# Six of nine input projections by one level of Strassen's product, with weight sums formed in DRAM

## Chip, core and metric

The kernel runs on one core of one Trainium2 chip. TensorE (PE in the profile) multiplies, VectorE (DVE), ScalarE (ACT) and GpSimd (POOL) do the elementwise work, SyncE (SP) and POOL issue most of the DMAs, and all DMAs share the core's 16 DMA engines. The metric is device time of one launch in microseconds (us), the median of three runs.

## What is computed

The reference is one layer of a hybrid decoder on 1024 tokens of width 1024, with 16 learned meta tokens put in front. Cut to what matters here:

```
h = rmsnorm(concat(meta, x))                       # 1040 x 1024
glu_a, glu_b, z, q, f, i, g_rec, m_conv, m_rec = split(h @ W_in)    # nine projections, 1024 x 1024 each
y_conv = (silu(layernorm(dwconv31(glu_a * sigmoid(glu_b)))) * silu(z)) @ W_conv_out
y_rec  = (group_rmsnorm(hgrn2(q, f, i)) * gnorm_g * silu(g_rec)) @ W_rec_out
x = x + (sigmoid(m_conv) * y_conv + sigmoid(m_rec) * y_rec) @ W_out
out = rmsnorm(x) * final_g
```

All of it is float32. hgrn2 is a gated linear recurrence over 8 heads.

## The kernel before, in words

Activations lie transposed: features on the 128 partitions, tokens along the row, eight k-tiles `hh[k]` of 1040 columns. A float32 product is made of three matmuls on rounded parts: every operand x is split into `hi` (x rounded to the type float32r) and `lo` = x - hi, and a product is hi·hi + hi·lo + lo·hi. `project` (L292 on) computes one 128-wide output tile over all tokens: for each column block it runs 8 k-tiles times these three matmuls (L300, L303, L304) into one PSUM bank. Tiles that also need the meta tokens (f, glu_a, glu_b) use the blocks `FB` of 348, 346 and 346 columns, the others `RB`, two blocks of 512.

The program is a list of jobs, one per output tile, and each job is a generator. In order of the program: v quarter 0 and 1 (from x itself, before the norm is known), then for head j = 0..7 the tiles f_j and q_j, with v quarter 2 after head 1 and v quarter 3 after head 3; then glu_b and glu_a of tile 0, and then, mixed by a counter, the eight g_rec tiles (`g_job`), the m_rec tiles with the W_rec_out tiles (`mr_job`, `ro_job`) and the other seven glu pairs; then z with the layer norm's statistics, m_conv (`mc_job`), W_conv_out (`co_job`), and last the product with W_out, whose lines are L907 to L909.

Each weight tile is loaded by SP in one DMA of 512 KB (`load_w`, L136), rounded by ACT (L126), negated by ACT (L127), and `lo` is completed by a DMA of POOL that adds the raw weights onto it in place (`split_dma`, L128, "wlo<-wraw"). Two raw buffers and three split buffers make a lookahead of one job.

Two background queues are advanced while matmuls are issued. `tick` takes a step of `hgrn` (the recurrence of one head: matmuls of tile "hg", DVE products) every `HG_GAP` us of matmul work, and `CONV_RATE` steps of `conv_taps` per us, each a DVE operation of 1024 columns (L612); `hgrn` ends with the normalised output `o_n` (L508), and `g_job` transposes it (L643). All the gates (m_rec, z, m_conv) stay in SBUF slots until they are used. The order of each engine's instructions is fixed when the program is built; an engine works through its own in that order and waits where an operand is not there.

Of the kernel before, what the change touches and what calls it, by code (L numbers as in the profile page):

```python
# [33 lines left out]
LN_AT = 3  # L34


@with_exitstack
def hybrid_kernel(ctx: ExitStack, tc: tile.TileContext, xT, xtok, wv, wp, wro, wco, wout, prm, fg, msk, out):
# [5 lines left out]
    qx = ctx.enter_context(tc.tile_pool(name="qx", bufs=2))  # L44
    wpool = ctx.enter_context(tc.tile_pool(name="wpool", bufs=3))
# [105 lines left out]
    def load_x(k):  # L151
# [6 lines left out]
        cuts = (0, NM + 2 * P, L) if k == 0 else (0, L)  # L158
# [22 lines left out]
    def v_mm(ps, k, c, ws, hi, lo, pair, first, last, shared):  # L181
# [6 lines left out]
        if c < NC:  # L188
            p0 = NM + c * P
# [31 lines left out]
    for c in range(NC):  # L221
        pe.matmul(pb[:, c:c + 1], lhsT=s2[:, NM + c * P:NM + (c + 1) * P], rhs=inv[:, 0:1], start=True, stop=True)
# [66 lines left out]
    for b, ps in enumerate(bcast_tok(diag_tok(rtok[:, 0:8]))):  # L289
        act.copy(out=rbc[:, NM + b * 512:NM + (b + 1) * 512], in_=ps)  # L290

    def project(w, xh, xl, blocks):  # L292

        whi, wlo = w
        res = []
        for o, n in blocks:
            ps = mm_bank()
            for k in range(KT):
                ks = slice(k * P, (k + 1) * P)
                mm = pe.matmul(ps[:, 0:n], lhsT=whi[:, ks], rhs=xh[k][:, o:o + n], start=(k == 0), stop=False)  # L300
                if not res and k == 0:
                    marks.append(mm)
                pe.matmul(ps[:, 0:n], lhsT=whi[:, ks], rhs=xl[k][:, o:o + n], start=False, stop=False)  # L303
                pe.matmul(ps[:, 0:n], lhsT=wlo[:, ks], rhs=xh[k][:, o:o + n], start=False, stop=(k == KT - 1))  # L304
                unit[0] = 3 * n / 2400.0
                if k < KT - 1:
                    yield None
            res.append(ps)
            yield o, n, ps

    on = [None] * NC
# [36 lines left out]
    def hgrn(j, Fg, K, QD):  # L348
# [21 lines left out]
        PA = slot("PA")  # L370
# [12 lines left out]
        QY = qx.tile([P, 7, 256], F32, name="QY", tag="qx")  # L383
        QY4 = QY.rearrange("p s (b u) -> p s b u", u=8)
# [102 lines left out]
        o_n = slot(f"o{j}", T)  # L487
        on[j] = o_n
# [22 lines left out]
        done.add(j)  # L511


    hh, hl, hpair = [], [], []
    jobs = []

    def normalise():
        hs = []
        for k in range(KT + 1):
            if k < KT:  # L520
# [3 lines left out]
                hs.append(h)  # L524
                hh.append(slot(f"hh{k}", dt=F32R))
# [7 lines left out]
    done = set()  # L533

    def f_job(j):
        def run(w):
            Fg = slot("F")
            K = slot("K")
# [14 lines left out]
    def q_job(j):  # L553
        def run(w):
            QD = qx.tile([P, 3, 512], F32, name="QD", tag="qx")
            for blk in project(w, hh, hl, RB):
# [4 lines left out]
                h0 = (o - NM) // 2  # L561
# [17 lines left out]

    def gb_job(j):  # L580
        def run(w):
            sg = slot("gsig")
# [9 lines left out]
    def ga_job(j):  # L592
        def run(w):
            a = glu.pop(j)
            for blk in project(w, hh, hl, FB):
                yield
                if blk is None:
# [3 lines left out]
            cj = slot(f"c{j}", T)  # L601
            conv[j] = cj
            dve.tensor_scalar(out=cj, in0=a[:, NM:L], scalar1=cw[:, j, TAPS - 1:TAPS], scalar2=conv_b[:, j:j + 1],
                              op0=ALU.mult, op1=ALU.add)
            cbg.append(conv_taps(j, a, cj))
# [18 lines left out]

    def c_reload():
# [5 lines left out]
    rh, rl = [], []  # L631

    def g_job(j):
        def run(w):
            while j not in done:
                step(bg)
            rec = slot("rec", T)
            po = []
            for b in range(2):
                ps = hg_bank()  # L640
                for c in range(4):
                    s = (4 * b + c) * P
                    pe.transpose(ps[:, c * P:(c + 1) * P], on[j][:, s:s + P], ident)  # L643
                po.append(ps)
            i = -1
            for blk in project(w, hh, hl, RB):
                yield
                if blk is None:
                    continue
                o, n, ps = blk  # L650
                i += 1
                sg = rec[:, i * 512:(i + 1) * 512]
                act.activation(out=sg, in_=ps, func=AF.Silu)
                dve.scalar_tensor_tensor(out=rec[:, i * 512:(i + 1) * 512], in0=po[i], scalar=gnorm[:, j:j + 1],
                                         in1=sg, op0=ALU.mult, op1=ALU.mult)
            hi = slot(f"rh{j}", T, F32R)
            lo = slot(f"rl{j}", T, F32R)
            split(rec, hi, lo)
            rh.append(hi)
            rl.append(lo)  # L660
        return run

    gate = {}
    grec_d = dram.tile([KT, P, T], F32, name="grec_d")
    c_d = dram.tile([KT, P, T], F32, name="c_d")
    gmc = {}

    def mr_job(j):
        def run(w):
            sm = slot("smr", T)  # L670
            for blk in project(w, hh, hl, RB):
                yield
                if blk is None:
                    continue
                o, n, ps = blk
# [197 lines left out]
    for _ in nrm:  # L873
        pass
# [158 lines left out]
```

## Time and profile before

| | us |
|---|---|
| median of 3 runs | 1233.21 (1232.68 to 1233.66) |
| the profiled execution | 1233.92 |
| its span, first to last instruction | 1231.9 |
| PE busy in it | 1203.6 |
| DVE busy | 753.3 |
| ACT busy | 420.6 |
| POOL busy | 140.7 |

The profile is of one execution. Busy time of an engine is the time in which it has an instruction running; matmuls overlap, so a matmul's own duration is longer than its pitch, the distance from one start to the next. "DMA share" is the mean busy share of the 16 DMA engines in a stretch.

### The profile page before, as it was taken

How to read it: one execution, taken by the hardware profiler on the slowest of the kernel's cores; microseconds unless marked ns; L12 is line 12 of the kernel's file. 1: busy time of each engine (PE TensorE's matmuls, PEld its weight loads, DVE VectorE, ACT ScalarE, POOL GpSimd, SP SyncE). 2: the span in 40 equal slices, each digit the busy share in tenths (PEclk: the TensorE clock that was granted, in tenths of full speed). 3: DMA queues.
4: the chain of work that ended last, by engine and by line, in shares of the span. 5: the costliest groups of instructions: out<-in, count | busy, mean ns of one | idle time of the engine just before them, and what ended most of it. 6: DMA issues, size and time to landing. Idle time of an engine off the chain costs nothing.

```text
span 1231.9 us, 19297 instructions
## 1 busy us (share of the span) xinstructions
PE 1203.6 (98%) x8136; PEld 1048.3 (85%) x8136; DVE 753.3 (61%) x1232; ACT 420.6 (34%) x722; POOL 140.7 (11%) x187
## 2 busy tenths in 40 slices
PE   8999999999999999999999999999999999999997
PEld 7988898997888889898989898888878788888886
DVE  7555736736766894778695969587651601435444
ACT  7553233343334333233222222221352824332211
POOL 5330010010001001010011101101100000110000
PEclk9999999999999999999999999999999999999999
DMA  5242142132222233343544444444634244654421
GB/s 217 84 115 58 36 103 69 36 85 69 55 69 70 54 83 94 97 103 86 138 107 115 120 120 103 133 107 127 183 87 100 65 106 103 162 130 161 147 86 52
DMA packets 35383, 124.22 MB, mean 101 GB/s; under 512 B 3936, under 2 KB 4320, under 8 KB 35296
## 3 DMA queue, kind: packets, MB, share of 16 engines
q0 software_dynamic: 17440, 63.51, 23.5%
q1 hardware_dynamic: 17712, 59.32, 14.0%
q8 instruction: 64, 1.05, 0.3%
q14 instruction: 23, 0.19, 0.1%
q10 hardware_dynamic: 144, 0.16, 0.0%
HBM read 67.40 MB, written 11.53 MB: 64 GB/s over the span
## 4 chain that ended last, share of the span: by engine, by line
PE 89%; DVE 8%; ACT 1%; issue 1%; DMA 0%; SPq 0%; DVEq 0%; ACTq 0%
PE mm L300 23%; PE mm L303 23%; PE mm L304 23%; PE mm L191 2%; PE mm L193 2%; PE mm L192 2%; PE mm L908 1%; PE mm L907 1%; PE mm L909 1%; PE hg L907 1%; PE hg L908 1%; PE hg L909 1%; PE hg L480 1%; PE hg L497 1%; PE hg L496 1%; DVE QX L367 1%
## 5 line engine op out<-in xcount | busy, mean ns | idle before, releaser
L300 PE MATMUL mm<-hh,whi 128*128 128x512 f32 (+2 forms) x1216 | 443.0, 365 | 0.0
L303 PE MATMUL mm<-hl,whi 128*128 128x512 f32 (+2 forms) x1216 | 439.5, 361 | 0.0
L304 PE MATMUL mm<-hh,wlo 128*128 128x512 f32 (+2 forms) x1216 | 438.1, 360 | 0.0
L612 DVE SCALAR_TENSOR_TENSOR c<-gsig,pt,c 128x1024 f32<-128x1024 f32 (+7 forms) x240 | 307.2, 1280 | 6.8
L300 PEld LDWEIGHTS mm<-hh,whi 128*128 128x128 f32 x1216 | 229.5, 189 | 29.4 <-ACT whi L126 0.5
L304 PEld LDWEIGHTS mm<-hh,wlo 128*128 128x128 f32 x1216 | 229.3, 189 | 28.0
L303 PEld LDWEIGHTS mm<-hl,whi 128*128 128x128 f32 x1216 | 229.4, 189 | 27.7 <-issue 0.5
L126 ACT CAST whi<-wraw 128x1024 fp32r<-128x1024 f32 x84 | 88.1, 1049 | 362.3 <-PE mm L303 349.1
L128 POOL DMA_DIRECT2D wlo<-wraw x84 | 73.1, 870 | 740.2 <-ACT wlo L127 651.1
L127 ACT ACTIVATE wlo<-whi 128x1024 fp32r<-128x1024 f32 x84 | 88.6, 1055 | 0.9
L600 DVE TENSOR_TENSOR gsig<-gsig,mm 128x346 f32<-128x346 f32 (+1 forms) x24 | 12.4, 516 | 84.8 <-PE mm L304 84.8
L565 DVE TENSOR_TENSOR QD<-mm,QD 128x512 f32<-128x512 f32 x16 | 18.0, 1123 | 59.4 <-ACT QD L564 59.4
L123 DVE TENSOR_TENSOR cl<-sz,ch 128x1024 fp32r<-128x1024 f32 x8 | 9.4, 1221 | 67.3 <-ACT ch L122 67.3
L304 PE MATMUL mm<-rh,wlo 128*128 128x512 f32 x128 | 50.5, 394 | 0.0
L300 PE MATMUL mm<-rh,whi 128*128 128x512 f32 x128 | 50.4, 394 | 0.0
L303 PE MATMUL mm<-rl,whi 128*128 128x512 f32 x128 | 50.4, 394 | 0.0
L303 PE MATMUL mm<-cl,whi 128*128 128x512 f32 x128 | 50.3, 394 | 0.0
L304 PE MATMUL mm<-ch,wlo 128*128 128x512 f32 x128 | 50.1, 393 | 0.0
L300 PE MATMUL mm<-ch,whi 128*128 128x512 f32 x128 | 50.0, 393 | 0.0
L191 PE MATMUL mm<-whi,xhi 128*128 128x256 f32 x112 | 33.0, 302 | 5.5 <-ACT xhi L162 5.5
L191 PE MATMUL mm<-whi,hh 128*128 128x256 f32 x128 | 37.5, 293 | 0.0
L192 PE MATMUL mm<-wlo,hh 128*128 128x256 f32 x128 | 36.0, 281 | 0.0
(261 smaller groups left out, 1701.0 us busy)
## 6 DMA issues: line engine op xcount, KB each, us to landing
wlo<-wraw POOLq DMA_DIRECT2D x84, 512.0 KB, 4.6
wraw<-in_wp_dram SPq DMA_DIRECT2D x64, 512.0 KB, 3.3
wraw<-in_wro_dram SPq DMA_DIRECT2D x8, 512.0 KB, 3.4
grec_d<-smr POOLq DMA_DIRECT2D x8, 512.0 KB, 3.0
wraw<-in_wco_dram SPq DMA_DIRECT2D x8, 512.0 KB, 3.3
gr<-grec_d POOLq DMA_DIRECT2D x8, 512.0 KB, 6.3
wraw<-in_wout_dram SPq DMA_DIRECT2D x8, 512.0 KB, 3.7
xt<-in_xtok_dram POOLq DMA_DIRECT2D x8, 512.0 KB, 5.8
```

What stands on the lines that cost most here:

```text
L126: act.copy(out=hi, in_=src)
L127: act.activation(out=lo, in_=hi.bitcast(F32), func=AF.Copy, scale=-1.0)
L128: nc.gpsimd.dma_start(out=lo, in_=src, accum_op=ALU.add)
L191: pe.matmul(ps, lhsT=a, rhs=whi, start=first, stop=False, **kw)
L192: pe.matmul(ps, lhsT=a, rhs=wlo, start=False, stop=False, **kw)
L193: mm = pe.matmul(ps, lhsT=b, rhs=whi, start=False, stop=last, **kw)
L300: mm = pe.matmul(ps[:, 0:n], lhsT=whi[:, ks], rhs=xh[k][:, o:o + n], start=(k == 0), stop=False)
L303: pe.matmul(ps[:, 0:n], lhsT=whi[:, ks], rhs=xl[k][:, o:o + n], start=False, stop=False)
L304: pe.matmul(ps[:, 0:n], lhsT=wlo[:, ks], rhs=xh[k][:, o:o + n], start=False, stop=(k == KT - 1))
L612: dve.scalar_tensor_tensor(out=dst, in0=a[:, p0 - d:L - d], scalar=cw[:, j, TAPS - 1 - d:TAPS - d], in1=dst, op0=ALU.mult, op1=ALU.add)
L907: pe.matmul(ps, lhsT=a, rhs=whi, start=(k == 0), stop=False)
L908: pe.matmul(ps, lhsT=a, rhs=wlo, start=False, stop=False)
```

## The change

The two projections that the same hidden tokens feed are taken in pairs: glu_b with glu_a, g_rec with m_rec, z with m_conv. For a pair and a tile j, the weights form a 2 x 2 block matrix (projection by upper and lower half of the 1024 features), the activations another (feature half by token half). One level of Strassen's product in Winograd's form gives the four blocks from 7 block products where the plain way takes 8. `strassen` runs the seven, each of 4 k-tiles times the three matmuls, and combines them with TT (elementwise operations of DVE) on PSUM and on work tiles; `put` is handed the four results and turns them into gates.

Weight sums: each pair needs four sums of weight blocks, 128 x 512 each (256 KB). `weight_sums` forms them in DRAM: for each batch of two or three tiles four copies DRAM to DRAM on SP's queue (L714), and four DMAs on POOL's queue that add onto them (L716), in three dependent stages. 23 pairs (glu 1 to 7, rec 0 to 7, z 0 to 7) make 11 batches, 44 copies and 44 additions.

Activation sums: `normalise` also writes h to DRAM (L552); at the beginning of the Strassen part `h_sums` loads it again, forms four combinations per k on DVE (L796 to L799) and splits them with ACT and POOL's adding DMA.

Gates and outputs: rec (the normalised recurrence output times silu(g_rec)), sigmoid(m_rec), silu(z), sigmoid(m_conv) go to DRAM and come back when used; the transposes of o_n moved from `g_job` into the end of `hgrn` (L535), whose result goes to DRAM too. The token axis has 16 columns twice (1056 columns, two halves of 528), so f and glu 0 now use four blocks of 264, 264, 256 and 256 columns. The order of parts is now: f, q, v and glu 0, all recurrence steps and weight sums drained, then 23 Strassen units, then W_rec_out, layer norm, W_conv_out and the last product.

```diff
-FB = ((0, 348), (348, 346), (694, 346))
-RB = ((16, 512), (528, 512))
-SLOTS = 37
+FB = ((0, 264, 0), (264, 264, 264), (LH + NM, 256, LH), (LH + NM + 256, 256, LH + 256))
+RB = ((NM, 512, 0), (LH + NM, 512, 512))
+SLOTS = 35
-HG_GAP = 2.1
-CONV_RATE = 0.7
-GLU_OVER = 22
+HG_GAP = 1.85
+CONV_RATE = 0.57
+SUM_GAP = 3.6
+GLU_OVER = 15
...
+        count[2] += unit[0]
+        if count[2] >= SUM_GAP:
+            count[2] = 0.0
+            step(sbg)
...
+            s = [sums[kind][i, j0:j1].rearrange("j p n -> p j n") for i in range(4)]
+            a = {(r, h): blk(kind, r, h, j0, j1) for r in range(2) for h in range(2)}
+            batches.append((
+                ((s[0], a[1, 0]), (s[2], a[1, 0]), (s[1], a[0, 0]), (s[3], a[0, 1])),
+                ((s[0], a[1, 1]), (s[2], a[0, 0])),
+                ((s[1], s[0]),),
+                ((s[3], s[1]),)))
+        for t in range(len(batches) + 3):
+            for st in range(4):
+                if 0 <= t - st < len(batches):
+                    for dst, src in batches[t - st][st]:
+                        if st == 0:
+                            nc.sync.dma_start(out=dst, in_=src)
+                        else:
+                            nc.gpsimd.dma_start(out=dst, in_=src, accum_op=ALU.add)
+                        yield
...
+    drain(bg)
+    drain(sbg)
+    first.close()
...
+    def h_sums():
+        for k in range(4):
+            ha, hb = slot("ha"), slot("hb")
+            nc.sync.dma_start(out=ha, in_=h_d[k])
+            nc.sync.dma_start(out=hb, in_=h_d[k + 4])
...
+            TT(out=t56[:, 0], in0=b11, in1=b12, op=ALU.subtract)
+            TT(out=t56[:, 1], in0=t56[:, 0], in1=b22, op=ALU.add)
+            TT(out=t74[:, 0], in0=b22, in1=b12, op=ALU.subtract)
+            TT(out=t74[:, 1], in0=t56[:, 1], in1=b21, op=ALU.subtract)
+            for i, src in ((6, t56[:, 1]), (5, t56[:, 0]), (4, t74[:, 1])):
+                t = slot(f"t{i}_{k}", dt=F32R).rearrange("p (a n) -> p a n", a=2)
+                split_dma(src, t[:, 0], t[:, 1])
+                tt[i].append(t)
+            split_dma(t74[:, 0], hh[k][:, LH:LX], hl[k][:, LH:LX])
...
+        def product(i, ps, mov, start=True):
+            whi, wlo = take(m0 + i)
+            for c, (o, n) in enumerate(cols):
+                for k in range(4):
+                    a, b = whi[:, k * P:(k + 1) * P], wlo[:, k * P:(k + 1) * P]
+                    xh, xl = (m[:, o:o + n] for m in mov(k))
+                    mm = pe.matmul(ps[c], lhsT=a, rhs=xh, start=start and k == 0, stop=False, skip_group_check=True)
...
+                    pe.matmul(ps[c], lhsT=a, rhs=xl, start=False, stop=False, skip_group_check=True)
+                    pe.matmul(ps[c], lhsT=b, rhs=xh, start=False, stop=k == 3, skip_group_check=True)
...
+        yield from product(0, X, b11)
...
+        yield from product(1, W, tcomb(6))
...
+        yield from product(2, X, b21, False)
...
+        yield from product(3, Y, t7)
...
+        yield from product(4, Z, tcomb(5))
...
+        yield from product(5, Y, tcomb(4), False)
...
+        yield from product(6, Z, b22, False)
```

How the engines' orders move, at the places that matter. First the beginning of SP's queue, where x and the first weights are loaded ("x" is the input, "wraw" raw weights). Before:

```order
L136 DMA wraw<-in_wv_dram 128x768
L160 DMA x_122<-in_xT_dram 128x1040
L160 DMA x_131<-in_xT_dram 128x1040
L136 DMA wraw<-in_wv_dram 128x1024
L160 DMA x_146<-in_xT_dram 128x1040
L160 DMA x_155<-in_xT_dram 128x1040
```

And with the change:

```order
L147 DMA wraw<-in_wv_dram 128x768
L714 DMA sum_rec<-in_wp_dram 128x2x512 x2
L171 DMA x_122<-in_xT_dram 128x1056
L714 DMA sum_rec<-in_wp_dram 128x2x512 x2
L171 DMA x_131<-in_xT_dram 128x1056
L147 DMA wraw<-in_wv_dram 128x1024
L714 DMA sum_glu<-in_wp_dram 128x2x512
L171 DMA x_146<-in_xT_dram 128x1056
L714 DMA sum_glu<-in_wp_dram 128x2x512 x2
```

The copies of the weight sums stand between the loads of x, and all 44 of them stand ahead of the load of q_2's weights. Second, POOL's queue from the splits of q_1 to those of f_2 ("wlo<-wraw" is the adding DMA that completes a weight's low part). Before:

```order
L128 DMA wlo<-wraw 128x1024 x2
L459 COPY km<-K 128x32
L355 MEMSET attnd 128x256
L128 DMA wlo<-wraw 128x1024 x2
L353 MEMSET attn 128x1024
```

With the change, where the first split shown is that of the second half of v quarter 2 and the last that of f_2:

```order
L716 DMA sum_z<-in_wp_dram 128x2x512 x2
L716 DMA sum_z<-sum_z 128x2x512
L716 DMA sum_rec<-sum_rec 128x2x512
L477 COPY km<-K 128x32
L716 DMA sum_z<-in_wp_dram 128x2x512 x2
L372 MEMSET attnd 128x256
L716 DMA sum_z<-sum_z 128x2x512 x2
L139 DMA wlo<-wraw 128x1024
L716 DMA sum_z<-in_wp_dram 128x2x512 x2
L716 DMA sum_z<-sum_z 128x2x512 x5
L370 MEMSET attn 128x1024
L139 DMA wlo<-wraw 128x1024
```

All 44 additions now stand ahead of the split of f_2's weights, 18 of them ahead of that of f_0. Third, DVE behind the last block of glu 0 ("c_5339" is the convolution of tile 0, "on" the normalised output of head 7, "ha" and "hb" the reloaded h), with the change:

```order
L112 TENSOR_TENSOR rt_o<-rt_o,rh_o 128x8
L645 SCALAR_TENSOR_TENSOR c_5339<-glu,pt,c_5339 128x1024
L113 SCALAR_TENSOR_TENSOR ro<-rt_o,ry_o 128x8
L645 SCALAR_TENSOR_TENSOR c_5339<-glu,pt,c_5339 128x1024
L525 TENSOR_TENSOR on<-hg,ro 128x512 x2
L645 SCALAR_TENSOR_TENSOR c_5339<-glu,pt,c_5339 128x1024 x3
L645 SCALAR_TENSOR_TENSOR c_5339<-glu,pt,c_5339 128x1023
L796 TENSOR_TENSOR t_5434<-ha 128x528
L798 TENSOR_TENSOR t_5435<-hb,ha 128x528
L797 TENSOR_TENSOR t_5434<-t_5434,hb 128x528
L645 SCALAR_TENSOR_TENSOR c_5339<-glu,pt,c_5339 128x1022
L799 TENSOR_TENSOR t_5435<-t_5434,hb 128x528
```

Before, that work on DVE held nothing of PE: its order behind the last matmuls of head 7 ("S", "Q") was

```order
L496 MATMUL hg<-v_2503,attn 128x128
L300 MATMUL mm<-hh_681,whi 128x512
L497 MATMUL hg<-S,Q 128x128
L303 MATMUL mm<-hl_682,whi 128x512
L304 MATMUL mm<-hh_681,wlo 128x512
```

with the transposes of head 7's output some 600 matmuls later, inside its g_rec tile. With the change it is

```order
L514 MATMUL hg<-S,Q 128x128
L535 MATMUL hg<-ident,on 128x128 x8
L841 MATMUL hg<-hh_582,wh 128x512
L844 MATMUL hg<-hl_583,wh 128x512
L845 MATMUL hg<-hh_582,wl 128x512
```

The transposes of head 7's output, which waits for DVE, now stand ahead of the first Strassen matmul. From the start of that convolution (one L613) to the "on" rows DVE has 13 convolution steps (L645) and 12 small operations of eight columns, from there to the last of the 16 operations of `h_sums` another 17 convolution steps.

## Rows read from the trace of the kernel before

**Rows 1.** The page: busy time of the engines, and the chain's shares by engine.

```profile
PE 1203.6 (98%) x8136; PEld 1048.3 (85%) x8136; DVE 753.3 (61%) x1232; ACT 420.6 (34%) x722; POOL 140.7 (11%) x187
PE 89%; DVE 8%; ACT 1%; issue 1%; DMA 0%; SPq 0%; DVEq 0%; ACTq 0%
```

**Rows 2.** PE's timeline in three stretches, start and duration in us first.

```profile
979.67 0.39 PE L300 MATMUL mm<-hh,whi 128*128 128x512 f32 x1
...
983.85 0.40 PE L300 MATMUL mm<-hh,whi 128*128 128x512 f32 x1
...
70.13 0.32 PE L303 MATMUL mm<-hl,whi 128*128 128x346 f32 x1
...
73.93 0.32 PE L303 MATMUL mm<-hl,whi 128*128 128x346 f32 x1
...
54.55 0.28 PE L193 MATMUL mm<-whi,xlo 128*128 128x256 f32 x1
...
57.95 0.28 PE L192 MATMUL mm<-wlo,xhi 128*128 128x256 f32 x1
```

**Rows 3.** Windows: busy us by engine, granted clock, DMA share, GB/s.

```profile
core 0: us, PE busy (x) PEld busy (x) DVE busy (x) ACT busy (x) POOL busy (x), PEclk, DMA share, GB/s
0.00:62.00 62.00, 56.24 (x430) 53.92 (x431) 40.39 (x58) 39.40 (x68) 30.15 (x38) 1.00 0.43 149
0.00:160.00 160.00, 149.16 (x1463) 138.53 (x1464) 98.64 (x195) 77.77 (x155) 44.73 (x57) 1.00 0.34 98
```

**Rows 4.** Line L192 between 118 and 166 us: v quarter 2.

```profile
L192 PE MATMUL mm<-wlo,hh x64: 276/280/293, 121.3 to 156.3; 128*128 128x256 f32 x64
```

**Rows 5.** Windows around one adding DMA, one weight load, and the loads of x.

```profile
456.00:460.00 4.00, 4.00 (x19) 3.24 (x18) 4.00 (x5) 1.85 (x3) 0.00 (x0) 1.00 0.69 131
460.00:464.00 4.00, 4.00 (x19) 3.24 (x18) 3.93 (x5) 0.00 (x0) 0.00 (x0) 1.00 0.37 133
10.00:15.00 5.00, 5.00 (x30) 4.89 (x30) 4.07 (x4) 5.00 (x6) 2.88 (x4) 1.00 1.03 421
```

**Rows 6.** The page's DMA issues: KB each, us from issue to landing.

```profile
wlo<-wraw POOLq DMA_DIRECT2D x84, 512.0 KB, 4.6
```

**Rows 7.** DVE's timeline at 575 us, then groups: busy us, mean ns.

```profile
574.96 11.84 DVE L612 SCALAR_TENSOR_TENSOR c<-gsig,pt,c 128x1024 f32<-128x1024 f32 x9
L600 DVE TENSOR_TENSOR gsig<-gsig,mm 128x346 f32<-128x346 f32 x16 | 8.3, 516 | 49.0 <-PE mm L304 49.0
L603 DVE TENSOR_SCALAR c<-gsig,pt 128x1024 f32<-128x1024 f32 x8 | 6.5, 813 | 0.3
L101 DVE TENSOR_TENSOR rt_o<-rt_o,rh_o 128x8 f32<-128x8 f32 x24 | 4.0, 165 | 0.6
L508 DVE TENSOR_TENSOR o<-hg,ro 128x512 f32<-128x512 f32 x16 | 10.3, 685 | 0.4
L449 DVE TENSOR_TENSOR K<-K,PA 128x512 f32<-128x512 f32 x16 | 11.0, 690 | 10.3 <-PE hg L443 9.5 <-PE hg L435 0.8
L122 ACT CAST mh<-gr 128x512 fp32r<-128x512 f32 x16 | 9.8, 615 | 42.0 <-DVE gr L790 42.0
```

**Rows 8.** Window from head 6 to the last product.

```profile
300.00:1060.00 760.00, 755.67 (x4471) 652.30 (x4470) 498.20 (x632) 255.02 (x377) 71.23 (x93) 1.00 0.40 102
```

More of the change, by code (lines that the diff above doesn't have):

```diff
@@ L524, in normalise @@
                 hs.append(h)
+                nc.gpsimd.dma_start(out=h_d[k], in_=h)
                 hh.append(slot(f"hh{k}", dt=F32R))
@@ new lines, in add_pair, with add_plain, take_tile @@
+    def add_pair(kind, j, fn):
+        units.append((len(pieces), fn))
+        a = {(r, h): wp[SECT[kind][r], j][:, h * 512:(h + 1) * 512] for r in range(2) for h in range(2)}
+        s = [sums[kind][i, j] for i in range(4)]
+        pieces.extend([a[0, 0], s[1], a[0, 1], s[2], s[0], a[1, 1], s[3]])
+    def add_plain(srcs, fn):
+        units.append((len(pieces), fn))
+        for src in srcs:
+            pieces.extend([src[:, 0:512], src[:, 512:1024]])
+    def take_tile(m):
+        a, b = take(m), take(m + 1)
+        return (a[0], b[0]), (a[1], b[1])
@@ L625, in c_reload, with rec_reload @@
+    rh, rl = [], []
+    def rec_reload():
+        for k in range(KT):
+            r = slot(f"r{k}", T)
+            nc.sync.dma_start(out=r, in_=rec_d[k])
+            hi, lo = slot(f"rh{k}", T, F32R), slot(f"rl{k}", T, F32R)
+            split_dma(r, hi, lo)
+            rh.append(hi)
+            rl.append(lo)
     def c_reload():
@@ L629, in c_reload @@
             conv[j] = cj
[L631 to L660, printed above, removed]
-        return run
@@ L663, in hybrid_kernel @@
[L663 to L675, printed above, removed]
-                act.activation(out=sm[:, o - NM:o - NM + n], in_=ps, func=AF.Sigmoid)
-            gate[j] = sm
-        return run
@@ L870, in hybrid_kernel @@
-    for i, _ in enumerate(v1):
-        if i % 6 == 0:
-            next(nrm, None)
-    for _ in nrm:
-        pass
-    def execute(job):
-        fn, w = job
-        for _ in fn(w):
-            tick()
-    pending = None
-    for srcs, fn in jobs:
-        ws = [load_w(s) for s in srcs]
-        if pending is not None:
-            execute(pending)
-        pending = (fn, ws[0] if len(ws) == 1 else ws)
-    execute(pending)
+    order = []
+    nglu = 1
+    for i in range(16):
+        order.append(("rec", i) if i < 8 else ("z", i - 8))
+        if (i + 1) * 7 // GLU_OVER >= nglu and nglu < KT:
+            order.append(("glu", nglu))
+            nglu += 1
@@ new lines, in hybrid_kernel @@
+    for kind, j in order:
+        if kind == "glu":
+            add_pair(kind, j, glu_unit(j))
+        elif kind == "rec":
+            add_pair(kind, j, gate_unit(rec_d, gmr_d, j, True))
+        else:
+            add_pair(kind, j, gate_unit(sz_d, gmc_d, j, False))
+    add_plain([], simple(rec_reload))
+    add_plain([wro[0], wro[1]], ro_first(0))
+    add_plain([], simple(c_reload))
+    for j in range(2, KT):
+        if j == LN_AT:
+            add_plain([], simple(lambda: drain(cbg)))
+            add_plain([], simple(ln_stats))
+        if j == LN_AT + 3:
+            add_plain([], simple(ln_var))
+        if j == LN_AT + 4:
+            add_plain([], simple(ln_bcast))
+            add_plain([], simple(ln_apply))
+        add_plain([wro[j]], ro_unit(j))
@@ L890, in hybrid_kernel @@
+    for j in range(KT):
+        add_plain([wco[j]], co_unit(j))
+    h_sums()
+    for m0, fn in units:
+        for _ in fn(m0):
+            tick()
     fgt = slot("fgt", T)
```

456 lines of the change are left out of this document (305 added, 151 removed).

## Prediction

> **What bounds the kernel now.** I read the page first: PE is busy for 98% of the span, and 89% of the chain that ended last runs through it [rows 1]. The busy time alone would not prove a bound, because matmuls overlap, so the second view is PE's timeline, where the pitch shows [rows 2]. The 512-column matmuls start 18 pitches apart in 4.18 us, 0.2322 us each; 24 pitches of 346 columns take 3.80 us, 0.1583 each; 29 of 256 columns take 3.40 us, 0.1172 each. They follow each other without a hole, so a matmul that is left out gives its pitch back, as long as nothing else becomes late. The third view is the windows. From 300 to 1060 us PE is busy for 755.67 of 760 us, with DVE at 498 us and a DMA share of 0.40 [rows 8]; there PE is the bound and all else has room. The first 160 us are the part to study for this change: there the DMA share is 0.34 [rows 3], so of 160 us the 16 engines are idle for 106 and busy for 54. The reader should keep that 106.
>
> **The matmuls removed.** A rec or z pair takes 96 matmuls of 512 columns now and 84 then: 12 x 0.2322 = 2.79 us, times 16 pairs is 44.6 us. A glu pair takes 144 matmuls of 346 (22.80 us) and then 168 of 264. No row has 264 columns; between the rows of 256 and 346 the pitch is 0.1172 + 8 x 0.0411 / 90 = 0.121 us, so 20.31 us; 2.49 x 7 = 17.4 us. The ten f and glu 0 tiles go from 72 x 0.1583 = 11.40 us to 48 x 0.121 + 48 x 0.1172 = 11.43: +0.3 us in all. The transposes of the heads are moved, not added. **Sum on PE: -61.7 us**, all of it in stretches where PE is the bound.
>
> **The weight sums added.** 23 pairs x 4 sums x 256 KB are 24.1 MB copied DRAM to DRAM and 24.1 MB added onto DRAM, each as much as 46 DMAs of 512 KB. The price of such a DMA is not in the trace, because none goes from DRAM to DRAM. The nearest rows are windows with one DMA in them [rows 5]: an adding DMA of 512 KB from SBUF to SBUF holds all 16 engines for 0.69 x 4 = 2.76 us, a load of 512 KB for 0.37 x 4 = 1.48 us. At these prices: 46 x 1.48 + 46 x 2.76 = 195 us. The other end comes from the traffic: the most that the trace shows DRAM deliver is 421 GB/s, at a DMA share of 1.03 [rows 5]. A copy reads and writes a byte, an addition reads two and writes one, so 24.1 x 2 + 24.1 x 3 = 120.5 MB at 421 GB/s is 286 us. To either comes h written to DRAM, eight times 541 KB, 12 us.
>
> What that costs is decided by where it stands. In the new order all 44 additions stand on POOL's queue ahead of the split of f_2's weights, and 43 of the 44 copies ahead of their load on SP's, so PE cannot begin f_2 before nearly all of it is through. Now f_2 begins behind the last matmul of v quarter 2, at 157 us or a little later [rows 4]; I take 160. Up to there 106 us of DMA time are idle. If every idle moment is filled, the delay is 195 + 12 - 106 = 101 us by the low price and 286 + 12 - 106 = 192 us by the high one. No row decides between them: the low price leaves out that both ends are in DRAM, the high one that reads alone were measured. I take the middle, **+147 us**. A part shows early. 18 additions and 17 copies stand ahead of f_0, which needs 27 us of DMA time now (0.43 of 62, [rows 3]); with 18 x 2.76 + 17 x 1.48 = 75 us more and the first h it is ready at about 107 us at the low price, not 62. The copies also stand between the loads of x, in a stretch where the engines are full already [rows 5].
>
> The Trainium skill says more of a copy's price: the page "DMA: Bandwidth & Descriptors", section "Latency and other measured facts", has copies between HBM tensors at 207 to 214 GB/s in each direction. No run here shows that; my estimate from the page is 24.1 MB / 0.21 = 115 us for the copies where the load's row gives 68, and a delay of 148 us where the low end gives 101.
>
> **The start of the Strassen part.** Here the new order makes PE wait for DVE. Behind PE's last glu 0 matmul DVE has the evacuation (0.52), the start of the convolution (0.81), 13 convolution steps of 11.84 / 9 = 1.31 us, 12 small operations of 0.165 and the two "o" operations of 0.69 [rows 7]: 0.5 + 0.8 + 17.0 + 2.0 + 1.4 = 21.7 us. PE has about one us of work in that time, eight small matmuls, and then the transposes that need "on". Wait: 20 us. Before, the same DVE operations stood there and the transposes far later, so nothing waited. Then DVE has 17 more convolution steps (22.3 us) and the 16 sums of h_sums (16 x 0.69 = 11.0) before the last t is formed; two ACT operations of 0.62 [rows 7] and an adding DMA that lands in 4.6 us [rows 6] follow: 39 us. PE can do three products that need no sum and three quarters of four that do, 36 + 36 = 72 matmuls, 16.7 us. Wait: 22 us. **Together +43 us**, on the path by PE's order. Below, it could be 20, if the sums are formed earlier than I read; above, hardly more than 50.
>
> **The rest.** A rec pair then takes PE 84 x 0.2322 = 19.5 us. In that time DVE has some ten convolution steps (13.4) and seven operations of 0.69 (4.8), 18.2 us, and the DMA engines seven half-size pieces at (1.48 + 2.76) / 2, four stores of half size and one load, 14.8 + 3.0 + 1.5 = 19.3 us. What had room [rows 8] is now within 7% of PE in three places. Waits will appear; I book 10 us for the section and the reload of rec, with 0 and 46 (a tenth of the section's 458 us) as ends. In W_conv_out the normalised tiles come from DVE in about 2.4 us each, and two tiles' matmuls, mixed by k, use one in 2.8 us: nothing.
>
> **The sum** is made against the profiled execution, 1233.9 us (2 us beside its span; the median of the runs is 0.7 us less): 1233.9 - 61.7 + 147 + 43 + 10 = **1372 us**.
>
> **Rivals.**
> *The sums are hidden, and it is faster.* They are needed only by the first products, after all of f, q and v, and the engines are idle for two thirds of the first 160 us. Against it: f_2 stands behind them in POOL's queue, and the prices. The point from which it decides: copy and addition of 512 KB together below (106 - 12) / 46 = 2.04 us, where the rows give 4.24. Then 1233.9 - 61.7 + 43 + 10 = 1225 us. 9%.
> *The sums delay, but the start of the Strassen part does not wait*, because the long waits for weights let DVE and the loads run ahead. Against it: the convolution starts only behind PE's last glu matmul. 1372 - 43 = 1329 us. 8%.
> *The Strassen units are bound by DMA or DVE, not by PE.* For it: 19.3 and 18.2 us against 19.5, and the sums' pieces arrive as bursts of seven. Then another 45 us: 1417 us. 13%.
> *Fewer matmuls than seven for eight are saved*: excluded, since the new order holds 84 and 168 per unit.
>
> **How the numbers follow.** My forecast has 70%; its own range, by the two prices, is 1326 to 1417 us. The range that should hold the time 8 times in 10 reaches down past the second rival to cheap sums and a short start, and up past the third: 1255 to 1455 us. A measurement of this kernel tells about 0.2% from no change. Faster by more: the first rival's, nearly all of its 9%, 8%; within 0.2%: 1%; slower: 91%.
>
> **What would show it.** In the changed profile: a DMA share near 1 over the first 200 us and more; PE waiting for wlo's DMA at f_0 and above all at f_2, which begins past 250 us; nothing of the kind after it; then PE waiting for DVE's "on" and for t6, t5, t7 for some 40 us; pitches as before, 0.232 for 512 columns and about 0.121 for 264; and a rec unit in 19.5 to 21 us. The prediction is wrong if f_2 begins before 200 us (the sums are cheaper than both prices), if the PE's wait at the first transposes is under 10 us, or if units take over 22 us.

## The result, and the profile after

The changed kernel takes 1419.2 us (median of 4, 1416.5 to 1421.3), the kernel before 1232.95 in the same session: ratio 1.151 [1.149, 1.153]. It is slower, by 186 us; the prediction had 1372 (1255 to 1455). The profiled execution took 1416.5 us. First its page: PE's busy time, granted clock and DMA share in 40 slices of 35.4 us.

```profile
PE 1204.5 (85%) x8352; PEld 1030.4 (73%) x8352; DVE 835.0 (59%) x1422; ACT 624.4 (44%) x1130; POOL 317.6 (22%) x410
...
PEclk8677877999999999659999999999998799999999
DMA  9998999552042212999999999999999897656331
```

PE was busy for 1203.6 us before [rows 1] and for 1204.5 now, although some 60 us of matmuls are gone: a first hint that the remaining ones became slower. The clock row says where: in the first seven slices and at two later places. The windows show the stages (columns as in [rows 3]).

```profile
0.00:160.00 160.00, 84.31 (x538) 78.16 (x538) 53.82 (x76) 50.36 (x83) 50.96 (x80) 0.76 1.00 269
160.00:260.00 100.00, 71.61 (x815) 62.56 (x816) 42.83 (x114) 22.36 (x52) 27.75 (x28) 0.80 1.07 238
260.00:560.00 300.00, 283.46 (x3270) 257.44 (x3269) 171.04 (x464) 110.40 (x293) 26.10 (x41) 1.00 0.29 73
560.00:640.00 80.00, 38.82 (x106) 24.05 (x105) 52.63 (x65) 38.85 (x74) 27.98 (x33) 0.66 0.90 218
640.00:1074.00 434.00, 434.00 (x2427) 377.53 (x2426) 348.03 (x393) 295.89 (x468) 133.58 (x158) 1.00 0.97 236
1074.00:1140.00 66.00, 36.92 (x111) 26.41 (x110) 31.98 (x31) 25.82 (x33) 15.39 (x23) 0.77 0.92 241
1140.00:1200.00 60.00, 60.00 (x264) 48.04 (x263) 27.82 (x48) 20.53 (x28) 17.68 (x25) 1.00 0.79 215
1200.00:1240.00 40.00, 28.83 (x102) 20.80 (x101) 21.95 (x26) 18.88 (x22) 7.83 (x12) 0.89 0.71 211
```

Read them by the idle time of PE. In the first 160 us PE is idle for 76 where it was idle for 11 [rows 3], with a DMA share of 1.00 for 0.34. From 260 to 560 all is well. Then come 41 idle us at the start of the Strassen part, none at all in its 434 us, 29 at the reload of rec and 11 ahead of W_conv_out. Who PE waits for, whole span (total, times, longest):

```profile
PE hg L206 <- POOL xpair L217: 43.3, 4, 17.9
PE mm L1002 <- DMA rl<-r: 28.0, 6, 9.4
PE hg L535 <- DVE on L525: 22.5, 4, 17.4
PE mm L322 <- DMA wlo<-wraw: 16.8, 2, 11.8
PE mm L203 <- DMA wlo<-wraw: 14.0, 1, 14.0
PE mm L318 <- ACT ch L133: 10.6, 4, 3.2
PE hg L844 <- DMA t<-t: 10.1, 5, 5.4
```

The first row was not in the forecast: small casts of POOL (xpair, for the meta tokens of v quarter 0) stand in POOL's queue among the additions, and PE waits for them. Here POOL holds a cast back while an addition waits for its copy and the next for that addition, and PE's matmul starts when the cast is through (POOL's timeline, then PE's):

```profile
46.40 1.14 POOL L716 DMA_DIRECT2D sum_glu<-sum_glu  x1 [11.95 <-DMA sum_glu<-in_wp_dram]
56.74 1.14 POOL L716 DMA_DIRECT2D sum_glu<-sum_glu  x1 [9.00 <-DMA sum_glu<-sum_glu]
57.43 0.65 POOL L217 CAST xpair<-xlo 128x16 fp32r<-128x16 f32 x1
58.13 0.42 PE L206 MATMUL hg<-whi,xpair 128*32 128x256 f32 x1 [17.80 <-POOL xpair L217]
```

L203 is v quarter 2, whose weights stand behind all but the last seven of the 44 additions; the two waits at L322 are for the weights of f_0 (4.9 us) and q_0 (11.8). The chain of waits runs through these (start, duration):

```profile
199.95 27.83 DMA sum_z<-sum_z
228.98 14.26 DMA wlo<-wraw
```

Behind v quarter 2's matmuls, and with no wait of its own, f_2's first matmul starts at 281 us (line L318 between 243 and 300 us: count, duration in ns, first and last start):

```profile
L318 PE MATMUL mm<-hh,whi x41: 279/285/398, 281.1 to 299.4; 128*128 128x264 f32 x16, 128*128 128x256 f32 x16, 128*128 128x512 f32 x9
```

The second part of the loss is in no wait. PE's timeline behind the wait at the transposes, and in the middle of the section:

```profile
577.94 1.97 PE L535 MATMUL hg<-ident,on 128*128 128x128 f32 x8 [17.44 <-DVE on L525]
...
580.56 0.63 PE L845 MATMUL hg<-hh,wl 128*128 128x512 f32 x1
580.99 0.63 PE L841 MATMUL hg<-hh,wh 128*128 128x512 f32 x1
581.42 0.63 PE L844 MATMUL hg<-hl,wh 128*128 128x512 f32 x1
...
700.28 0.39 PE L841 MATMUL mm<-t,wh 128*128 128x512 f32 x1
700.51 0.40 PE L844 MATMUL mm<-t,wh 128*128 128x512 f32 x1
```

Behind the wait the 512-column matmuls start 0.43 us apart, later 0.23. The windows around the two stretches (columns as above) have a granted clock of 0.50 and 1.00:

```profile
578.00:582.00 4.00, 4.00 (x14) 3.52 (x15) 3.93 (x4) 1.37 (x2) 0.56 (x1) 0.50 0.73 221
698.00:702.00 4.00, 4.00 (x19) 3.23 (x18) 2.75 (x5) 2.76 (x6) 0.86 (x1) 1.00 0.91 184
```

So the first are at the lower level of the clock, 1.2 GHz, after PE has stood still for 17.4 us. I took the whole timeline apart: for each matmul the idle time ahead of it, and the part of its pitch that lies above the pitches of [rows 2]. Before: 15 us idle, 31 of slow pitches. After: 196 idle, 92 of slow pitches, and 1121 us of matmuls at full pitch instead of 1181. **181 idle + 61 slow pitches - 60 matmuls = 182 us**, the difference of the two spans. The added slow pitches alone are as much as the Strassen product saves. Most of them are the clock: some 53 of the 92 us lie in stretches of granted clock 0.5, where before it was 3 of 31. "Lost" below is idle time and slow pitches together, by stage; e2 to e11 are the experiments of the next section. A column and those 1121 us together fall 2 to 6 us short of the span, so a difference of a few us between two columns shows nothing.

| lost, us | after | e2 | e3 | e4 | e6 | e5 | e8 | e9 | e10 | e11 |
|---|---|---|---|---|---|---|---|---|---|---|
| up to glu 0's last matmul ("phase one") | 160 | 46 | 61 | 164 | 166 | 174 | 59 | 57 | 54 | 49 |
| wait at the last transposes | 18 | 18 | 18 | 5 | 5 | 18 | 5 | 5 | 5 | 5 |
| first 62 us of the Strassen part | 39 | 40 | 45 | 44 | 30 | 41 | 42 | 30 | 29 | 30 |
| rest of the 23 units | 2 | 2 | 9 | 7 | 4 | 4 | 7 | 4 | 3 | 3 |
| reload of rec, first W_rec_out pair | 40 | 38 | 36 | 39 | 39 | 19 | 21 | 20 | 18 | 22 |
| behind it | 29 | 28 | 29 | 28 | 30 | 28 | 30 | 28 | 26 | 26 |

The kernel before loses 36 us in its first 600 and 46 in all. Behind the reload some 19 stand at the start of W_conv_out; 8 at the very end are in both kernels.

### The profile page after: what moved, and what is told of

Same layout as the page of the kernel before. It is cut to its first block, busy times and chain, and to the rows that moved or that the text cites. A ratio compares the mean times of both kernels' runs of the same rounds, so it can differ in the third digit from the quotient of the medians.

```text
span 1414.7 us, 21797 instructions
## 1 busy us (share of the span) xinstructions
PE 1204.5 (85%) x8352; PEld 1030.4 (73%) x8352; DVE 835.0 (59%) x1422; ACT 624.4 (44%) x1130; POOL 317.6 (22%) x410
## 4 chain that ended last, share of the span: by engine, by line
PE 61%; DMA 19%; DVE 9%; issue 6%; POOL 2%; ACT 2%; SPq 1%; DVEq 0%; POOLq 0%; ACTq 0%
PE mm L318 6%; PE mm L321 6%; PE mm L322 6%; PE hg L844 5%; PE hg L841 5%; PE hg L845 5%; PE mm L845 5%; PE mm L844 5%; PE mm L841 5%; DMA wlo<-wraw 2%; DMA sum_rec<-in_wp_dram 2%; DMA sum_z<-sum_z 2%; DMA sum_rec<-sum_rec 2%; DMA r<-rec_d 2%; DVE c L645 2%
## 5 line engine op out<-in xcount | busy, mean ns | idle before, releaser
L645 DVE SCALAR_TENSOR_TENSOR c<-glu,pt,c 128x1024 f32<-128x1024 f32 (+7 forms) x240 | 307.0, 1279 | 4.9
L139 POOL DMA_DIRECT2D wl<-wr x193 | 166.6, 896 | 430.9 <-ACT wl L138 410.8
L322 PE MATMUL mm<-hh,wlo 128*128 128x264 f32 (+2 forms) x448 | 145.8, 326 | 16.8 <-DMA wlo<-wraw 16.8
L318 PE MATMUL mm<-hh,whi 128*128 128x264 f32 (+2 forms) x448 | 148.8, 333 | 7.1 <-ACT v L270 6.5
L321 PE MATMUL mm<-hl,whi 128*128 128x264 f32 (+2 forms) x448 | 145.7, 326 | 1.0 <-DVE hl L557 0.9
L322 PEld LDWEIGHTS mm<-hh,wlo 128*128 128x128 f32 x448 | 87.3, 195 | 23.7 <-DMA wlo<-wraw 17.5
L318 PEld LDWEIGHTS mm<-hh,whi 128*128 128x128 f32 x448 | 87.7, 196 | 13.6 <-ACT v L270 6.8
L321 PEld LDWEIGHTS mm<-hl,whi 128*128 128x128 f32 x448 | 87.5, 195 | 7.1 <-DVE hl L557 1.7
L844 PE MATMUL hg<-t,wh 128*128 128x512 f32 (+1 forms) x180 | 64.5, 358 | 10.1 <-DMA t<-t 10.1
L841 PE MATMUL hg<-t,wh 128*128 128x512 f32 (+1 forms) x180 | 63.4, 352 | 5.8 <-ACT t L137 5.0
L844 PE MATMUL mm<-t,wh 128*128 128x512 f32 (+1 forms) x180 | 63.0, 350 | 0.0
L841 PE MATMUL mm<-t,wh 128*128 128x512 f32 (+1 forms) x180 | 62.6, 348 | 0.0
```

The costliest lines, as they stand in the source:

```text
L139: nc.gpsimd.dma_start(out=lo, in_=src, accum_op=ALU.add)
L318: mm = pe.matmul(ps[:, 0:n], lhsT=a, rhs=xh[k][:, o:o + n], start=(k == 0), stop=False)
L321: pe.matmul(ps[:, 0:n], lhsT=a, rhs=xl[k][:, o:o + n], start=False, stop=False)
L322: pe.matmul(ps[:, 0:n], lhsT=b, rhs=xh[k][:, o:o + n], start=False, stop=(k == KT - 1))
L645: dve.scalar_tensor_tensor(out=dst, in0=a[:, p0 - d:L - d], scalar=cw[:, j, TAPS - 1 - d:TAPS - d], in1=dst, op0=ALU.mult, op1=ALU.add)
L841: mm = pe.matmul(ps[c], lhsT=a, rhs=xh, start=start and k == 0, stop=False, skip_group_check=True)
```

## The experiments

Each time is of one run beside a run of the kernel before (1231.8 to 1232.5 us).

**e1, the price of the sums' DMAs.** A kernel of DMAs only.

> Not the layer at all: only DMAs of 512 KB, in four stages one after the other (24 copies DRAM to DRAM, 24 additions DRAM onto DRAM, 24 additions SBUF onto SBUF, 24 loads); the layer's work is left out and the output means nothing. In the changed kernel the 16 engines are busy for 1.02 x 260 = 265 us of the first 260, before for 0.34 x 160 = 54 of the same work, and h adds 12; so 46 copies with 46 additions hold them for about 199 us, 4.3 us per pair. Theory A (the low price of the prediction was right, both ends in DRAM cost no more): copy about 1.5 us, addition about 2.8 us each, the same as the load and the SBUF addition beside them. Theory B (the traffic price): 1 MB of traffic per copy and 1.5 MB per addition at 421 GB/s, copy 2.5 us, addition 3.7 us. Theory C (copies cost more than loads, additions less than between SBUF tiles): copy over 2.1, addition under 2.3.

Windows inside the four stages (DVE, POOL, clock, DMA share, GB/s): copies DRAM to DRAM, additions DRAM onto DRAM, additions between SBUF tiles, loads.

```profile
10.00:40.00 30.00, 0.00 (x0) 0.00 (x0) 1.00 1.00 322
50.00:110.00 60.00, 0.00 (x0) 23.27 (x21) 1.00 1.12 201
150.00:190.00 40.00, 0.00 (x0) 10.01 (x12) 1.00 1.06 200
210.00:230.00 20.00, 0.00 (x0) 0.00 (x0) 1.00 1.03 413
```

512 KB at these rates are 1.63, 2.61, 2.62 and 1.27 us. Theory A holds: an addition costs the same in DRAM as in SBUF, a copy 0.36 us more than a load. A pair costs 4.24 us, 46 pairs 195: the low price of the prediction, to the microsecond. That is in part luck: the copy was put at 1.48 us and the addition at 2.76, and the two errors cancel. The traffic bound is refuted: a copy at 322 GB/s reads and writes 644 GB/s together, above the 421 that I had taken for a limit.

**e2, no sums.**

```diff
-    sbg = [weight_sums()]
+    sbg = []
...
-        s = [sums[kind][i, j] for i in range(4)]
+        s = [a[1, 0], a[0, 0], a[1, 0], a[0, 1]]
```

> The weight sums are not formed; the products read plain weight blocks in their place, as many bytes, so the numbers of the outputs differ. Stage by stage the changed kernel loses against its own matmul pitches (idle time and pitches above those at full clock) 133 us before 260 us, where the kernel before lost 14: 119 us. Theory A (those 119 us all come from the sums): 1416.5 - 119 = 1298 us, f_2 begins at about 130 to 160 us, the clock in the first 160 us near 1.0. Rival B (half of it comes from the order of the POOL and SP queues, from h written to DRAM and from the longer x tiles, not from the sums): 1340 to 1360. Rival C (phase one then runs into the recurrence's DVE work and the time comes back later): above 1360.

1298.07 us: theory A. Its first 160 us look like those before [rows 3], clock included:

```profile
0.00:160.00 160.00, 148.80 (x1495) 137.61 (x1496) 98.99 (x199) 79.56 (x161) 43.59 (x66) 1.00 0.42 129
```

The sums cost 118 us; none of PE's waits for xpair or for "wlo<-wraw" is left, and f_2 starts at 165 us. Everything else of the loss (66 us over the kernel before, in spite of 60 us less matmuls) has other causes.

**e3, the same sums later.**

```diff
-SUM_GAP = 3.6
+SUM_GAP = 2.6
...
-                            nc.sync.dma_start(out=dst, in_=src)
+                            gated(nc.sync.dma_start(out=dst, in_=src), marks[-1])
...
-                            nc.gpsimd.dma_start(out=dst, in_=src, accum_op=ALU.add)
+                            gated(nc.gpsimd.dma_start(out=dst, in_=src, accum_op=ALU.add), marks[-1])
```

(`gated` orders a DMA behind another instruction, here the first matmul of the running job.)

> All 88 sum DMAs stay, but each is ordered behind the first matmul of the job that is running when its step comes, from f_0 on, one per 2.6 us of matmul work. Theory A (the place decides: what costs is that the additions stand ahead of f_2's weights and x): from 260 to 560 us the DMA share of the changed kernel is 0.29, so 213 us are idle for some 199 us of sums; the 119 us go to 10 to 40, 1310 to 1340 us, with some PE waits for wlo spread over the phase. Rival B (the volume decides, wherever it stands): DMA share near 1 over the whole phase, PE waiting for wlo again and again, 1390 to 1420 us.

1323.8 us, theory A: 93 of the 118 us come back with every byte still moved. The place decides, not the volume. Spreading the sums changes two things at once, what stands in the queues and how full the DMA engines are; their shares are not separated. The sums now lie under phase one:

```profile
0.00:160.00 160.00, 145.52 (x1453) 134.44 (x1454) 99.47 (x199) 77.91 (x151) 53.06 (x74) 0.99 0.73 211
160.00:460.00 300.00, 276.21 (x3173) 250.28 (x3172) 169.18 (x457) 105.59 (x282) 65.92 (x71) 0.98 0.75 174
```

A DMA share of 0.74 over 460 us with PE at 92%: where the share was 1.00, PE had half.

**e4, the convolution of tile 0 behind the activation sums.**

```diff
-            conv_start(j, a)
+            glu[j] = a
...
-    h_sums()
+    conv_start(0, glu.pop(0), h_sums())
```

(`h_sums` returns its last DVE operation, and the start of the convolution is ordered behind it.)

> The convolution of tile 0 (start and 30 steps, 41 us of DVE) begins behind the activation sums instead of ahead of them. The start of the Strassen part loses 57 us in the changed kernel: 19 at the transposes that wait for DVE's on, 22 idle for the t sums and 16 at the low clock. Theory A (DVE's queue is the cause): the wait at the transposes goes to 2 or less and the first t is formed some 20 us earlier; what stays is h's reload, its splits and their DMAs, 20 to 28 us; 1416.5 - 30 = 1386 us. Rival B (the sums of h are bound by the reload and the adding DMAs, not by DVE): only the 19 us go, 1397 us. Rival C (the 41 us of DVE come back in the section, where DVE is busy for up to 19.7 of 20 us, and ahead of the layer norm): 1410 to 1425 us.

1411.4 us: theory A fell, and the total lies in rival C's range. The wait at the transposes shrank from 17.4 to 4.4 us, as said. Of the t's that ACT rounds the first comes 16 us sooner (572.6 us for 588.2), but the last only 2 (620.5 for 622.8). PE's waits from 556 to 635 us now name DMAs instead:

```profile
PE hg L847 <- DMA t<-t: 14.4, 4, 5.6
PE hg L844 <- ACT t L137: 7.7, 2, 5.7
PE hg L847 <- DMA hl<-t: 4.8, 3, 2.8
PE hg L535 <- DVE on L525: 4.4, 1, 4.4
```

So of this boundary's 57 us DVE's queue caused 13. Some 5 of them came back in the next 62 us and some 5 in the section, where DVE now carries the 41 us; both are near what the table can tell.

**e6, also the activation sums split by DVE.** Two calls of `split_dma` in `h_sums` become `split`.

> As the kernel with the late convolution (1411.4 us, 43.5 us lost in the first 62 us of the Strassen part), with the low parts of the 16 activation sums formed by DVE subtractions (16 x 0.69 = 11 us) instead of 16 adding DMAs of 270 KB. Theory A (once DVE is free, the adding DMAs are the bound of that stretch: 16 x 1.35 = 22 us of the engines, beside 10 us for h's loads): the loss goes to 20 to 28, 1390 to 1396 us. Rival B (the loads of h are late, and DVE's sums wait for them): 36 to 44 lost, 1404 to 1412 us. Rival C (weight pieces are late): waits move to wh and wl, 1404 to 1412 us.

1399.4 us, 30 lost where e4 lost 44: between A and B. The adding DMAs were worth 13 us; what is left begins with h's loads, which DVE waits for (some of the waits from 556 to 625 us):

```profile
PE hg L844 <- ACT t L133: 16.4, 3, 7.9
DVE t L798 <- DMA ha<-h_d: 16.3, 3, 10.3
DVE t L799 <- DMA hb<-h_d: 5.2, 3, 2.0
```

**e5, the reload of rec without adding DMAs.** `split_dma(r, hi, lo)` becomes `split(r, hi, lo)`.

> Only the reload of rec differs: its low part is formed by a DVE subtraction instead of ACT's negation and an adding DMA. The stretch from the last Strassen matmul to the end of the first W_rec_out pair loses 40 us in the changed kernel (29 idle, 11 by pitches at the lower clock). Theory A (the DMA engines are the cause: eight adding DMAs at 2.6 us are 21 us there): the wait of rl on its DMA goes, the stretch loses 15 to 22, 1392 to 1400 us. Rival B (DVE still has some 19 convolution steps, 25 us, at that place, and the subtractions stand behind them): PE waits for DVE instead, 1410 to 1420 us. Rival C (the loads of rec are the cause, each landing 7 to 9 us late): no wait less, 1412 to 1418.

The stretch lost 18.7 us instead of 40.3, theory A, yet the time is 1411.25: phase one, whose POOL and SP orders are unchanged, lost 174 instead of 160. This stretch is not steady while the DMA engines are full: in five kernels with the sums in their first place it lost 160, 161, 164, 166 and 174. By the stage theory A holds; the total lies outside its range, in rival B's.

**e7, W_conv_out's first two tiles mixed by k.** A copy of `ro_first` for `ch` and `cl`.

> The first two W_conv_out tiles run mixed by k, as the first two of W_rec_out do, so PE has 12 matmuls (2.8 us) for each normalised tile instead of 3 (0.7 us). The rest behind the reload loses 28.8 us in the changed kernel, 11 of it idle before W_conv_out's matmuls and 9 by slow pitches right there. Theory A (PE overtakes ACT and DVE because a single tile uses up a k in 0.7 us): the wait for ch shrinks to 4 or less, 8 to 15 us less, 1402 to 1409 us. Rival B (the normalised tiles come every 5 us and more, because their loads of sz stand behind the weights' additions in POOL's queue): the wait stays within 3 us of 11, 1412 to 1418 us.

1416.3 us, wait 11.0: rival B's time. The wait is as long as before the edit (10.6); the normalised tiles arrive every 3.5 to 7.7 us. Whether sz's place in POOL's queue is the reason is asked again in e9.

**e8, together** (e3, e4, e6, e5's edit and e7's, and a faster pace of the convolution).

> Paced sums, late convolution of tile 0, activation sums and rec split by DVE, W_conv_out's first two tiles mixed, convolution pace 0.66 instead of 0.57 per us of matmul work; the result is the layer's. If the losses add up by stages: 1323.8 - 13 (transposes) - 20 (activation sums) - 20 (reload) - 10 (W_conv_out) = 1261 us, range 1245 to 1285. If the paced sums' DMA traffic and the added DVE work get into each other's way: 1290 to 1320. It would then still be slower than before (1232), by what phase one loses (61 us against about 35 without sums).

1291.3 us: 30 above the sum by stages, and in the other range that was given, for edits that get into each other's way. By the table 17 of the 30 are missing at the start of the Strassen part, 11 at W_conv_out, where e7's edit again gained nothing, and 5 at the reload. At the start of the Strassen part the paced sums end too late: their last additions hold POOL's queue, and the first Strassen weights wait behind them (POOL's timeline, then PE's).

```profile
456.40 1.14 POOL L718 DMA_DIRECT2D sum_z<-sum_z  x1 [8.02 <-DMA sum_z<-sum_z]
...
471.45 1.14 POOL L718 DMA_DIRECT2D sum_z<-sum_z  x1 [3.74 <-DMA sum_z<-sum_z]
472.14 4.08 POOL L139 DMA_DIRECT2D wl<-wr  x4
```

```profile
479.52 0.80 PE L848 MATMUL hg<-hh,wl 128*128 128x512 f32 x1 [14.06 <-DMA wl<-wr]
```

**e9, the sums sooner, h and sz in other queues.**

```diff
-SUM_GAP = 2.6
+SUM_GAP = 2.0
...
-            nc.sync.dma_start(out=ha, in_=h_d[k])
-            nc.sync.dma_start(out=hb, in_=h_d[k + 4])
+            nc.scalar.dma_start(out=ha, in_=h_d[k])
+            nc.scalar.dma_start(out=hb, in_=h_d[k + 4])
...
-            gated(nc.gpsimd.dma_start(out=sz, in_=sz_d[j]), marks[-2])
+            gated(nc.sync.dma_start(out=sz, in_=sz_d[j]), marks[-2])
```

> As the combination (1291.3 us) with three edits in three separate stages, read stage by stage, and without the mixed W_conv_out tiles, which moved nothing. First: a step of the sums per 2.0 us of matmul work instead of 2.6, so that the last additions, which hold POOL's queue from 447 to 472 us there while the first Strassen weights wait behind them (wl 14 us late), stand ahead of glu 0; second: h comes back through ACT's queue instead of SP's, where its loads of 489, 500 and 512 us stood behind weight loads that waited for a buffer. Theory A (queue order is the cause of the 42 us lost at the start of the section): 15 to 25 lost. Rival A2 (the DMA engines are): 32 or more, or the loss moves to phase one, which then loses 75 instead of 59. Third: the loads of sz stand in SP's queue instead of POOL's, where each stood behind an addition that waits for ACT's wl, and ACT for sz's own product. Theory B (that ring is the cause of the 19 us lost at W_conv_out's start): PE's wait for ch of 10 us falls to 5 or less. Rival B2 (the SBUF slots free too late for the loads): 8 or more stays. Total by A and B: 1255 to 1268 us; by the rivals 1280 to 1295.

1270.9 us, between the two ranges. The start lost 30 instead of 42, so A in part; which of its two edits did it (sums that end sooner, h in ACT's queue) the run does not separate, and e6 lost 30 there with h in SP's queue. sz's queue changed little (PE's wait for ch 8.5 after 10.0).

**e10, rec through ACT's queue, the layer norm 11 us earlier.**

> As the second combination (1270.9 us) with two edits in two stages. The loads of rec go through ACT's queue: in SP's queue seven of them stood between weight loads that wait for a buffer, and ACT waited 18.7 us for them. The layer norm's variance and broadcast stand one W_rec_out tile (11 us) earlier. Theory A (SP's queue order is what is left of the reload's 20 us): ACT's wait for r and PE's wait for rh (10.3 us) halve, the stretch loses 10 to 14. Rival A2 (the SBUF slots come free only with the last Strassen products): 18 to 21 lost. Theory B (the normalised tiles begin too late, behind 16 DVE products of 0.68 us): PE's wait for ch, 8.5 us there, goes to 4 or less. Rival B2 (each tile's chain DMA, DVE, ACT, DVE is what limits, by its loads): 7 or more stays. By A and B 1252 to 1260 us, by the rivals 1266 to 1272.

1262.2 us, but by neither edit: the reload lost 18 instead of 20 and the wait for ch was 9.3. By the stages both rivals, A2 and B2, describe it; the 9 us came in small pieces, the largest (3) in phase one. DVE waits for the loads of sz, and in SP's timeline each leaves right behind a weight load, while SP waits for buffers that the adding DMAs of earlier weights still hold (waits from 1040 to 1095 us, then SP's timeline):

```profile
DVE sz L1071 <- DMA sz<-sz_d: 19.4, 5, 7.4
SPq L775 <- DMA wl<-wr: 34.2, 7, 8.4
```

```profile
1066.70 0.33 SPq L775 DMA_DIRECT2D wr<-in_wco_dram  x1
1067.08 0.45 SPq L1070 DMA_DIRECT2D sz<-sz_d  x1
```

What holds the start of W_conv_out is left open: the tile order, POOL's queue and the start of the norm were each tried and are not it alone. In both queues that were tried the loads of sz stood behind the weights; no run took them out.

**e11, the same without sums.**

> As the third combination (1262.2 us), with the weight sums left out and plain weight blocks read in their place, so the numbers of the outputs differ. It asks what is left of the loss to the kernel before (30 us) when the sums are free. The third combination loses in all 135 us against its own pitches at full clock, the kernel before 51, for 60 us of matmuls saved: phase one 54, start of the Strassen part 34, section 3, reload 18, behind it 26. Theory A (paced, the sums still cost what phase one loses beyond the 46 us of the kernel without sums): 1262 - 8 = 1254 us. Rival B (the paced sums' DMA traffic is also behind the late h and weight loads at the start of the section): start of the section at 20 to 25 instead of 34, 1240 to 1247 us. Rival C (below 1232: the sums are still the whole difference).

1261.5 us, none of the three: with the order of e10 all 48 MB of sums cost 0.7 us, less than the runs of one kernel differ. By the table phase one gained 5, and the reload gave 4 back. The two stretches with the sums (e10) and without (e11):

```profile
0.00:160.00 160.00, 146.46 (x1459) 135.40 (x1460) 99.54 (x199) 77.92 (x151) 56.37 (x77) 0.99 0.81 230
160.00:460.00 300.00, 277.53 (x3174) 252.06 (x3173) 172.51 (x468) 110.87 (x293) 67.19 (x74) 0.98 0.75 174
```

```profile
0.00:160.00 160.00, 147.63 (x1481) 136.23 (x1482) 99.02 (x199) 79.16 (x159) 43.62 (x66) 1.00 0.41 129
160.00:460.00 300.00, 279.82 (x3167) 252.67 (x3165) 170.71 (x469) 112.70 (x290) 28.89 (x43) 0.98 0.28 71
```

No version beat the kernel before. The best that computes the layer, e10, is 30 us slower: it loses 135 us for 46, less the 60 us of matmuls. Most of what it loses more is at three boundaries where a stage begins from DRAM: 34 at the Strassen part, 18 at rec, some 18 at W_conv_out. The rest is in phase one (54 for 36).

## Why the prediction was right, and where it was off

Slower, by the mechanism named, and 44 us more than forecast: 1416.5 for 1372. That it came so near is in part luck: the sums were put 29 us too high, the start of the Strassen part and the rest 65 too low. Of the signs of a wrong prediction none showed in its sense: f_2 began past 250 us (281), the wait at the transposes was 17.4 us, and behind the first unit, which the start of the part stretches to 56 us, only rec and z units of at most 21.6 and glu units of 20.4 follow. Term by term:

**Matmuls, -61.7: right.** 60 us fewer at full pitch; a rec unit takes 19.6 us from its first matmul to the next unit's.

**Weight sums, +147: the mechanism right, the price too high; +118 by e2.** What holds PE is what was named, additions ahead of what it needs on POOL's queue, but not at the place: it waited 43 us for the casts of v quarter 0, which the text did not see in that queue, 5 and 12 for the weights of f_0 and q_0, 14 for those of v quarter 2, and not at all at f_2. f_0 starts at 125 us (107 by the low price), f_2 121 us later than the 160 I took. The step that failed in the sum is "I take the middle": the low price, from the nearest rows [rows 5], was exact, 4.24 us per pair, and the high one rested on reads alone. By the low price the delay was 101. The other 17 us were not traced one by one; the slow pitches that go with the sums are 22 us in phase one (45 after, 23 in e2), and PE still had v quarter 2's matmuls to run when its last weights came, at 243 us. The Trainium skill, page "DMA: Bandwidth & Descriptors", section "Latency and other measured facts", gave 207 to 214 GB/s for copies between HBM tensors, measured on tiles with rows of 16 KiB that no run here has. From it I had estimated 115 us for 46 copies of 512 KB; e1 has 322 GB/s, 75 us, and the measurement decides.

**Start of the Strassen part, +43: 57.** The wait for "on" was put at 20 and is 17.4; e4 shows the cause as named. The t sums were put at 22, and lost 39. The sum counted DVE's work, and e4 shows that this was not the chain: with the convolution out of the way the last t came only 2 us sooner. The sixteen adding DMAs are 13 us of it, by e6, on engines that were 0.90 busy; that the reload of h is the rest is argued from e6's waits and was not isolated.

**The rest, +10: 61. This is the step that failed most.** Its two ends (0 and 46) were about the section, which lost 2 us: at a DMA share of 0.97 PE waited for nothing. "The reload of rec" was named and not priced: eight loads and eight adding DMAs, 8 x (1.27 + 2.61) = 31 us of the engines where PE's matmuls give 8 x 2.8 = 22, from a start with nothing in SBUF. That is an estimate of a shortfall of 9; it lost 40, and e5 halves it by taking the additions out. And W_conv_out "nothing": it lost 19. The text had its tiles mixed by k, 2.8 us for each; only W_rec_out's first two are. But e7 mixes them and gains nothing, because the tiles come slower than the 2.4 us I gave them.

**No term at all: the clock.** Of the loss 61 us are slow pitches, some 50 of them in stretches of granted clock 0.5; each term in the sum was a wait's length alone. The Trainium skill, page "TensorE: Matmul & The Clock Gate", section "HAM oscillation — how this bites in real kernels", tells of a kernel whose matmuls start at half clock again after each wait for a DMA. The 0.43 us rows behind the 17.4 us wait agree, though that wait was for DVE.

118 + 57 + 61 - 60 is 177 of the 183 us between the two profiled executions; the other 6 are within the 10 by which phase one without the sums loses more than the kernel before (46 for 36), and were not traced further.

**The first rival, that the sums are hidden,** was given 9% with the condition that a pair costs below 2.04 us. The condition was wrong in kind: at 4.24 us they are hidden too (e10 against e11), if they are ordered over 450 us instead of the first 250. The place decided, not the price; how much of that is the order of the two queues and how much the full engines is not separated. Even so it would not have been faster: without any sums e2 takes 1298 us.

**The third rival, units bound by DMA or DVE,** had 1417 us, the measured time, but by chance: its units would have taken longer, and they take what PE needs, at a DMA share of 0.97.

**The second rival,** no wait at the start of the Strassen part, had 1329 us; that part lost 57.

## What to carry to other kernels

Work that is moved to DMAs has room only where its queue entries stand: spread it by order over the stretch whose share is low, and keep it out of the queue ahead of anything that PE needs soon. Price each boundary at which a stage starts from DRAM by itself, as loads, adding DMAs and PE's rate, not as a share of the section. And add to each wait of PE the slow matmuls behind it: here 61 us of slow pitches came with 181 us of idle time.

## What the runs showed of the hardware that was not expected

- In a row of its kind an adding DMA of 512 KB takes 2.61 us between DRAM tensors and 2.62 between SBUF tiles; a copy in DRAM 1.63, a load 1.27 (e1).
- The sums' two kinds of DMA, run together with loads, cost no more than apart: 1.02 x 260 us, less 54 and 12, is an estimate of 199 us for 195 by the prices.
- With the DMA engines full at the start, runs of the changed kernel spread over 4.8 us, those of the kernel before over 1.1.
